# Adding P1 onto C11: 56 accumulating transfers spread over the stages after P1

## The chip, the cores and the metric

The kernel runs on one core of a Trainium2 chip. The metric is the device time of one execution in microseconds. Times are taken over several executions; the profile is one execution that was recorded by the hardware profiler.

## The reference

Eight experts each multiply the same rows by their own weights, and the results are added with softmax probabilities as factors:

```python
batch, seq, hidden, n_experts, expert_hidden = 16, 512, 512, 8, 2048
probs = np.exp(router_logits - logits_max); probs = probs / np.sum(probs, axis=-1, keepdims=True)
for e in range(n_experts):
    output += probs[:, :, e:e+1] * np.matmul(x, expert_weights[e])
```

Scaling a row of `x` by an expert's probability ahead of the product gives the same sum, so the whole is one product: 8192 rows, 8 x 512 = 4096 terms (expert and hidden), 2048 columns. Inputs and output are f32.

## The kernel before

The large product is done as a Strassen-Winograd scheme. Rows are split into blocks of 256 (`HQ`): block 2q is the "even" half, 2q+1 the "odd" one, q from 0 to 15. Experts 0 to 3 and 4 to 7 are the two halves of the terms, and the columns are split into two halves of 1024 (`NH`). Seven products P1 to P7 with sums of operands replace eight. P1 + P2 is C11, the output rows of the even block in the first half of the columns. Within each product the same scheme is used again on tiles of 128 rows and 512 columns: seven steps, in the order 1, 5, 6, 2, 7, 3, 4 (`STEPS`), each of eight matmuls into one PSUM bank. In P1, P2 and P3 most stages are opened by a third level of the scheme (`by_thirds`), in steps of four matmuls.

The work is a list of stages, `stages`, made by hand. A stage takes one or two products of one or two q; with two products it has 14 steps, called slots 0 to 13 below. The order is: seven stages of P1 (q 2 to 15), eight of P2 (q 2, 3, 4, 5, 0, 1, 6, ... in pairs), then P6 with P5 (`k5` is the first), then P7, and P4 with P7 (`k7` is the stage of the last P6 and the first P7, the turn), then P3 (`k3` is the stage of the last P4), until `end`. `ND` is 7, the first P2 stage.

TensorE runs the steps in this order. VectorE makes the left operands (tiles `z`: rows of x, `xT`, times probabilities, `pT`) and their differences (`d`), the weight sums (`w`), and most of the additions out of PSUM (`ps`, `pt`) into 128 x 512 f32 tiles `h`. ScalarE copies from PSUM into `h`. Twelve `h` buffers go round; one is free again when the transfer that stores it has landed. Of the result, some parts are added to what was stored earlier: P7 loads such a base block from the output (`h<-out_dram`) into an `h` tile.

Three queues start transfers. SP loads `xT`, `pT`, base blocks and kept operands. ScalarE's queue fetches weight sums of 1 MB (`w<-wd`). POOL stores results to the output, loads and casts weights and rows, sends weight sums to DRAM, and issues every transfer that adds onto DRAM (`accum_op=ADD`). Each queue starts its transfers in program order. A POOL transfer also waits until the one eight before it on that queue has landed.

P1's result is needed in C11 and elsewhere, so it is kept in DRAM: `kept[q]`, two column blocks of 256 rows. For q 0 to 13 (`ON_BASE` is 14) P2 stores its own part of C11 to the output, and P1 is added to it later from `kept[q]`: four transfers of 128 x 512 f32 (256 KB) each for 14 q, 56 in all, read from DRAM and added onto DRAM. The profile names them `out_dram<-kept`, the function is `add_kept`, the line of POOL's transfers is L121. They depend on nothing but P2's stores and the stores of `kept`. The hooks put them among the steps: `at(stage, slot, make)` runs `make` ahead of that step while the program is written, so the transfer gets its place on POOL's queue behind the stores of all earlier steps. Before the change, the places come from one table row each for q 0 to 11 (from stage `k7 + 3`, one q every 15 slots) and q 12, 13 (from `k3 + 5`, every 14 slots).

Of the kernel before, what the change touches and what calls it, by code (L numbers as in the profile page):

```python
# [31 lines left out]
def kernel(  # L32
# [51 lines left out]
    with tc.tile_pool(name="psum0", bufs=1, space=bass.MemoryType.PSUM) as psum0:  # L84
        zero = h_tile([P, NB], f16)
        nc.vector.memset(zero, 0.0)
        every = psum0.tile([P, 8, NB], f32, name="every")
# [32 lines left out]
    def pool(o, i, **how):  # L120
        note(nc.gpsimd.dma_start(out=o, in_=i, **how))  # L121
# [506 lines left out]
    ND = 7  # L628
    ON_BASE = 14
# [27 lines left out]
    def at(stage, slot, make):  # L657
        hooks.setdefault((stage, slot), []).append(make)

    def add(*products):  # L660
        stages.append(products)
        return len(stages) - 1
# [36 lines left out]
    def product(r, q, **how):  # L699
        left, loads = left_of(r, q)  # L700
        lefts[r, q] = left
        p = None
        if r == 1:
            def sink(tn, o):
                pool(kept_rows(q)(tn), o)
            p = Product(right[1], left, sink)
        elif r == 2:
            if q >= ON_BASE:
                bases[2, q] = Base(kept_rows(q))
            p = Product(right[2], left, to_out(q, 0, 0), bases.get((2, q)))  # L710
        elif r == 5:
            bases[6, q] = m1 = Base(kept_rows(q))
            m1.task = {}

            p = Product(right[5], left, to_out(q, 1, 0))
        elif r == 6:
            m1 = bases[6, q]

            def base(tn):
                need(m1.task[tn])  # L720
                return m1.t[tn]
            p = Product(right[6], left, to_out(q, 0, 1), base)
        elif r == 7:
            base = bases[7, q] = Base(lambda tn: out_rows(q, 0, 1, tn))
            p = Product(right[7], left, to_out(q, 1, 1), base)
        elif r == 4:
            p = Product(right[4], left, to_out(q, 1, 0, accum_op=ADD), products[7, q].o.__getitem__)
        else:
            p = Product(right[3], left, to_out(q, 0, 1, accum_op=ADD), **how)
        p.loads = loads  # L730
        products[r, q] = p
        return p
# [131 lines left out]
    k5 = add(product(5, 0), product(5, 1))  # L864
# [3 lines left out]
    some = product(6, 15)  # L868
    xs.clear()
    k7 = add(some, product(7, 0))  # L870
    for q in range(15):
        add(product(4, q), product(7, q + 1))
    some = product(4, 15)
    xs.clear()
    k3 = add(some, product(3, KEPT_Z))
    for q in range(0, KEPT_Z, 2):
        add(product(3, q), product(3, q + 1))
    end = add(product(3, 15))
# [87 lines left out]
    for i, (kn, e) in enumerate((kn, e) for kn in (ODD, (0, 0), (1, 1), (1, 0)) for e in range(2)):  # L966
        stage = ND + i - 2 if kn != ODD else 2 + 2 * i
# [42 lines left out]
    def slots_after(stage, slot, n):  # L1010
        slot += n
        while slot >= 7 * len(stages[stage]):
            slot -= 7 * len(stages[stage])
            stage += 1
        return stage, slot
# [127 lines left out]
    def add_kept(q, n, t):  # L1143
        pool(out_f[ds(2 * q * HQ + t * HP, HP), ds(n * NB, NB)], kept[q][n, ds(t * HP, HP), :], accum_op=ADD)

    for first, stage, every in ((0, k7 + 3, 15), (12, k3 + 5, 14)):
        for n, q in enumerate(range(first, min(first + 12, ON_BASE))):
            for i in range(4):
                at(*slots_after(stage, 0, every * n + every * i // 4), lambda q=q, i=i: add_kept(q, i // 2, i % 2))

    finish = products[3, 15]
    finish.base = Base(lambda tn: out_rows(15, 0, 1, tn))
# [81 lines left out]
```

## Time and profile before

| | |
|---|---|
| median of 3 runs | 1361.7 us (1361.27 to 1362.39) |
| profiled execution | 1360.91 us, of which the span from first to last instruction is 1359.1 us |
| PE busy | 1352.8 us, 6846 matmuls |
| DVE (VectorE) busy | 1133.7 us |
| ACT (ScalarE) busy | 261.4 us |
| POOL (GpSimd) busy | 435.9 us, most of it issuing transfers |
| transfers `out_dram<-kept` | 56 of 256 KB, 56.9 us of POOL, median 9.0 us from issue to landing |
| transfers `out_dram<-h` on POOL | 380 of 256 KB, median 7.5 us to landing |
| first and last `out_dram<-kept` | issued at 844.6 and 1315.8 us |

The stages lie about so in the span: P1 to 212 us, P2 to 404 us, P6 and P5 to 792 us (from 768 us the turn to P7), P7 and P4 to 1155 us, P3 to 1350 us. Busy times of engines overlap. A group of the profile has the form "line engine operation out<-in"; a releaser is what ended an idle time. The DMA share is the mean busy share of the 16 DMA engines, and it can pass 1 where packets overlap.

### The profile page before, as it was taken

The numbers are of one execution on the slowest core, as the hardware profiler recorded it, in microseconds if no ns is written. First come the engines' busy times: TensorE is split into PE (matmuls) and PEld (weight loads), VectorE is DVE, ScalarE is ACT, GpSimd is POOL, SyncE is SP. The second block draws the span as 40 slices with busy tenths as digits, with TensorE's granted clock in tenths as the row PEclk, the third lists the DMA queues.
The fourth block names the chain that finished last, engine by engine and source line by source line (L and its number), as shares of the span: only waits on it lengthen the run. The fifth ranks groups of instructions, "written<-read, shape, count | busy, mean of one in ns | idle before, by whom it ended". The sixth has DMA issues, their size and how long they took to land.

```text
span 1359.1 us, 18757 instructions
## 1 busy us (share of the span) xinstructions
PE 1352.8 (100%) x6846; PEld 667.1 (49%) x6846; DVE 1133.7 (83%) x1374; ACT 261.4 (19%) x525; POOL 435.9 (32%) x667
## 2 busy tenths in 40 slices
PE   9999999999999999999999999999999999999998
PEld 4555555565544444444444444444444444556564
DVE  7877687878999888787887899988889897898884
ACT  3232423233211111111111100000000000224331
POOL 3223323333222332323312122453434443232342
PEclk9999999999999999999999999999999999999999
DMA  9899979888899999999997998999999999999997
GB/s 186 242 221 247 258 232 233 255 243 250 238 341 288 287 310 273 288 285 284 309 274 279 345 318 236 247 267 251 264 251 249 263 265 315 327 302 251 199 163 131
DMA packets 191116, 355.65 MB, mean 262 GB/s; under 512 B 53040, under 2 KB 81968, under 8 KB 186160
## 3 DMA queue, kind: packets, MB, share of 16 engines
q0 software_dynamic: 89824, 189.31, 59.6%
q1 hardware_dynamic: 97456, 139.86, 33.5%
q10 hardware_dynamic: 3744, 25.30, 4.7%
q8 instruction: 53, 0.87, 0.3%
q14 instruction: 39, 0.32, 0.1%
HBM read 210.53 MB, written 180.55 MB: 288 GB/s over the span
## 4 chain that ended last, share of the span: by engine, by line
PE 99%; DMA 0%; DVE 0%; issue 0%; POOL 0%; ACT 0%; POOLq 0%
PE ps L130 75%; PE pt L130 24%; DMA w<-in_x_dram 0%; DVE z L255 0%; POOL w L121 0%; DVE h L107 0%; ACT h L1180 0%; DVE lg L295 0%; POOLq L1218 0%
## 5 line engine op out<-in xcount | busy, mean ns | idle before, releaser
L130 PE MATMUL ps<-w,z 128*128 128x512 f16 (+1 forms) x3776 | 821.3, 374 | 0.0
L130 PEld LDWEIGHTS <-z 128*128 128x128 f16 x5264 | 515.0, 98 | 574.4
L121 POOL DMA_DIRECT2D out_dram<-h x380 | 256.7, 710 | 684.1 <-ACT h L617 269.5
L130 PE MATMUL pt<-w,z 128*128 128x512 f16 (+1 forms) x1488 | 312.7, 357 | 0.0
L107 DVE TENSOR_TENSOR z<-xT,pT 128x2048 f16<-128x2048 f16 x220 | 265.9, 1217 | 0.8 <-DMA xT<-xs 0.8
L107 DVE TENSOR_TENSOR h<-ps,h 128x512 f32<-128x512 f32 x250 | 170.2, 687 | 88.0 <-PE ps L130 67.2
L130 PE MATMUL ps<-w,d 128*128 128x512 f16 x880 | 199.1, 379 | 0.0
L604 ACT COPY h<-ps 128x512 f32<-128x512 f32 x118 | 69.2, 586 | 417.9 <-PE ps L130 385.3
L130 PEld LDWEIGHTS <-d 128*128 128x128 f16 x880 | 86.1, 98 | 99.8
L107 DVE TENSOR_TENSOR z<-z,d 128x2048 f16<-128x2048 f16 x110 | 131.8, 1216 | 0.0
L107 DVE TENSOR_TENSOR h<-pt,h 128x512 f32<-128x512 f32 x123 | 83.5, 686 | 43.3 <-PE pt L130 41.0
L107 DVE TENSOR_TENSOR w<-w 128x1024 f16<-128x1024 f16 (+2 forms) x104 | 110.2, 1075 | 1.9 <-PE ps L130 1.0
L617 ACT COPY h<-ps 128x512 f32<-128x512 f32 x50 | 29.3, 586 | 391.5 <-PE ps L130 387.1
L107 DVE TENSOR_TENSOR ps<-ps,h 128x512 f32<-128x512 f32 (+1 forms) x90 | 51.9, 579 | 28.5 <-PE ps L130 24.9
L107 DVE TENSOR_TENSOR d<-z 128x1024 f16<-128x1024 f16 x110 | 74.7, 684 | 1.1
L600 ACT COPY h<-ps 128x512 f32<-128x512 f32 x97 | 53.8, 604 | 69.4 <-PE ps L130 65.3
L121 POOL DMA_DIRECT2D kept<-h x56 | 30.6, 548 | 93.7 <-ACT h L604 52.6
L121 POOL DMA_DIRECT2D out_dram<-kept x56 | 56.9, 1058 | 11.2 <-DMA out_dram<-h 5.8
L596 ACT COPY ps<-ps 128x512 f32<-128x512 f32 x59 | 33.6, 570 | 120.7 <-PE ps L130 62.6
L107 DVE TENSOR_TENSOR ps<-pt,h 128x256 f32<-128x256 f32 x38 | 16.4, 432 | 41.5 <-PE pt L130 29.4
L107 DVE TENSOR_TENSOR h<-h 128x512 f32<-128x512 f32 (+2 forms) x69 | 45.1, 675 | 0.6 <-DMA out_dram<-h 0.4
L107 DVE TENSOR_TENSOR z<-z,u 128x2048 f16<-128x2048 f16 x36 | 44.1, 1225 | 1.2
(74 smaller groups left out, 558.6 us busy)
## 6 DMA issues: line engine op xcount, KB each, us to landing
out_dram<-h POOLq DMA_DIRECT2D x380, 256.0 KB, 7.5
pT<-p_dram SPq DMA_DIRECT2D x126, 256.0 KB, 7.7
w<-wd ACTq DMA_DIRECT2D x23, 1024.0 KB, 9.4
xT<-x SPq DMA_DIRECT2D x80, 256.0 KB, 7.7
h<-kept SPq DMA_DIRECT2D x72, 256.0 KB, 7.7
h<-out_dram SPq DMA_DIRECT2D x68, 256.0 KB, 6.7
w<-in_expert_weights_dram POOLq DMA_DIRECT2D x33, 512.0 KB, 10.3
kept<-h POOLq DMA_DIRECT2D x56, 256.0 KB, 6.0
```

The lines of the kernel that those rows point to most:

```text
L107: dve(nc.vector.tensor_tensor(out=o, in0=a, in1=b, op=op))
L121: note(nc.gpsimd.dma_start(out=o, in_=i, **how))
L130: note(nc.tensor.matmul(ps, z, w, start=start, stop=stop, skip_group_check=True))
L596: act(nc.scalar.copy(self.banks["b"], x))
L600: act(nc.scalar.copy(o[tn], q if p == 5 else x))
L604: act(nc.scalar.copy(o[TN[p]], b if p == 2 else x))
L617: act(nc.scalar.copy(o[tn], b))
```

## The change

The table of places is replaced. The 56 transfers are the same, on the same queue, with the same sources and targets. Their order is now q 2, 3, 4, 5, 0, 1, 6, ..., 13, the order in which P2 stores them, and the places are listed by stage and slot: two a stage in five stages of P2, two a stage in six of the stages of P6 with P5, alternately two and one a stage in P7 with P4 (from the first stage after the turn), two a stage in P3 from `k3 + 2`. 57 places are listed and the last is not used.

```diff
-    for first, stage, every in ((0, k7 + 3, 15), (12, k3 + 5, 14)):
-        for n, q in enumerate(range(first, min(first + 12, ON_BASE))):
-            for i in range(4):
-                at(*slots_after(stage, 0, every * n + every * i // 4), lambda q=q, i=i: add_kept(q, i // 2, i % 2))
+    added = [(q, i) for q in (2, 3, 4, 5, 0, 1, 6, 7, 8, 9, 10, 11, 12, 13) for i in range(4)]
+    places = [(stage, slot) for some, slots in (
+        (range(ND + 2, ND + 7), (3, 10)), ((k5 + 5, k5 + 7, k5 + 9, k5 + 10, k5 + 12, k5 + 13), (4, 11)),
+        (range(k7 + 1, k3, 2), (2, 9)), (range(k7 + 2, k3, 2), (6,)), (range(k3 + 2, end), (4, 10))) for stage in some for slot in slots]
+    for (q, i), where in zip(added, sorted(places)):
+        at(*where, lambda q=q, i=i: add_kept(q, i // 2, i % 2))
+    assert len(places) >= len(added)
```

The order of the instructions on TensorE, VectorE, ScalarE and SP is the same as before. On POOL it differs in the place of the adds alone. `kept_145` is the kept tile of q 2, `kept_143` that of q 0, `kept_144` of q 1, `kept_149` of q 6, `kept_148` of q 5.

POOL in a stage of P2, before:

```order
L121 DMA w<-in_expert_weights_dram 128x4x512 x2
L121 DMA wd<-u 128x2048
L121 DMA wd<-w 128x2048 x2
L121 DMA out_dram<-h 128x512 x8
L121 DMA w<-in_expert_weights_dram 128x4x512 x2
```

And with the change:

```order
L121 DMA w<-in_expert_weights_dram 128x4x512 x2
L121 DMA out_dram<-kept_145 128x512
L121 DMA wd<-u 128x2048
L121 DMA wd<-w 128x2048 x2
L121 DMA out_dram<-h 128x512 x4
L121 DMA out_dram<-kept_145 128x512
L121 DMA out_dram<-h 128x512 x4
```

One add now stands ahead of the sends of the weight sums, one amid the eight stores.

POOL from the end of P6 with P5 over the turn to P7 into P7 with P4, before (the stores are those of three stages and more):

```order
L121 DMA wd<-w 128x1024
L121 DMA out_dram<-h 128x512 x8
L121 DMA xs<-in_x_dram 128x2x512
L121 DMA out_dram<-h 128x512 x48
L121 DMA out_dram<-kept_143 128x512 x2
L121 DMA out_dram<-h 128x512
```

And with the change:

```order
L121 DMA xs<-in_x_dram 128x2x512
L121 DMA out_dram<-kept_144 128x512
L121 DMA out_dram<-h 128x512 x5
L121 DMA out_dram<-kept_144 128x512
L121 DMA out_dram<-h 128x512 x27
L121 DMA out_dram<-kept_144 128x512
L121 DMA out_dram<-h 128x512 x3
L121 DMA out_dram<-kept_144 128x512
L121 DMA out_dram<-h 128x512 x5
L121 DMA out_dram<-kept_149 128x512
```

Where 48 stores followed each other ahead of the first add, there are now adds ahead of the first store and after 5, 32, 35 and 40 of them. The add after 32 stores is the first in the stage after the turn; before the change the first add of all stands 16 stores behind that place.

## The prediction

> **What bounds the kernel now.** I read the page's busy row first, then the chain of waits, then the busy time by stage, since a mean over the whole span could hide an idle stretch where the adds stand. The first fence has the page's head, PE's busy tenths over 40 slices and the chain; the second has five windows that cover the program from P1 to P3 (columns: stretch, length, then busy time of PE, PEld, DVE, ACT and POOL, the granted clock, the DMA share, GB/s).
>
> ```profile
> span 1359.1 us, 18757 instructions
> ...
> PE   9999999999999999999999999999999999999998
> ...
> PE 99%; DMA 0%; DVE 0%; issue 0%; POOL 0%; ACT 0%; POOLq 0%
> ```
>
> ```profile
> 24.00:212.00 188.00, 188.00 (x1051) 101.97 (x1049) 146.34 (x175) 64.52 (x136) 53.11 (x88) 1.00 0.99 236
> 212.00:404.00 192.00, 192.00 (x1058) 103.25 (x1056) 159.07 (x186) 57.46 (x123) 55.86 (x97) 1.00 0.93 264
> 404.00:792.00 388.00, 388.00 (x1799) 175.90 (x1798) 324.76 (x392) 53.47 (x92) 106.52 (x188) 1.00 0.98 296
> 792.00:1155.00 363.00, 363.00 (x1683) 164.59 (x1682) 321.93 (x384) 17.59 (x30) 146.51 (x201) 1.00 1.02 262
> 1155.00:1350.00 195.00, 195.00 (x1099) 107.35 (x1097) 163.00 (x200) 61.14 (x132) 62.65 (x73) 1.00 1.00 235
> ```
>
> The windows are P1, P2, P6 with P5, P7 with P4, and P3. In every one the PE time equals the length of the stretch: TensorE has no idle time from 24 us to 1350 us, at the full clock. The start before 24 us and the stores after the last matmul hold no add. So in this execution there is nothing for another order of transfers to win; it can only lose, by making TensorE wait somewhere. The fourth row holds 48 of the 56 adds today, and even there PE is full. POOL is busy at most 146.51 of 363.00 us, so it has room for more issues in any stage.
>
> **The change, part by part.** No transfer is added or taken away; 56 adds of 256 KB leave their places and take others on the same queue. Their cost to POOL and their flight, from the view of the tile over 840 to 1150 us (min/median/max ns of the issue, then landing), beside the plain stores of P2:
>
> ```profile
> L121 POOL DMA_DIRECT2D out_dram<-kept x48: 805/916/1501, 844.6 to 1145.9; - x48
> ...
> DMA to landing us min/median/max: 5.7/9.0/14.9
> ...
> L121 POOL DMA_DIRECT2D out_dram<-h x32: 540/540/548, 264.5 to 346.7; - x32
> ...
> DMA to landing us min/median/max: 2.6/4.2/6.2
> ```
>
> POOL's queue. Counted in the new table, 10 adds go to P2, 12 to P6 and P5, 23 to P7 and P4, 11 to P3. The issues cost 10 x 0.92 = 9.2 us of POOL in P2, where 192.00 - 55.86 = 136 us are free, and 12 x 0.92 = 11 us in P6 and P5, where 388.00 - 106.52 = 281 us are free. P7 and P4 give back 25 x 0.92 = 23 us. What stands behind an add on POOL is a store of `out_dram`, a send `wd<-u` or, in P6 and P5, a part of a weight load; each goes out at most one add later, 0.8 to 1.5 us. Who waits for those stores is told by the view of the tile `out_dram`: for 264 to 352 us its part "who waited for it" is empty, so a store of P2 that lands in 4.2 us is not missed by anyone if it lands 1.5 us later. On ScalarE, which needs the `h` tiles that the stores give back, that stretch has these waits and no others, all on TensorE or VectorE:
>
> ```profile
> ACT h L604 <- PE ps L130: 45.9, 16, 8.0
> ACT ps L596 <- DVE ps L107: 9.0, 7, 1.9
> ACT h L600 <- PE ps L130: 3.1, 3, 1.0
> ```
>
> Term for P2: 0; if that cover were gone, 10 x 0.92 = 9.2 us. Term for P6 and P5: 0 by the same argument, but with less behind it: there the tile's view has some waits on the landing of a store.
>
> ```profile
> L121 POOL DMA_DIRECT2D out_dram<-h x107: 540/540/630, 406.3 to 719.0; - x107
> ...
>   ACT h L604: 19.5, 2
>   ACT h L600: 2.9, 1
> ...
>   DVE h L107: 1.5, 2
> ```
>
> ScalarE is busy 53 of 388 us there, and its two long waits (19.5 us together) stand in a run in which PE is full; so waits of 10 us on that side are covered. Uncovered, 12 x 0.92 = 11 us. The last add ahead of the turn to P7 stands in the third stage before it, and no add is placed in the turn itself, so the tight handover of weights there is left as it is.
>
> The two stages after the turn to P7. The present table leaves them free: its first add is at 844.6 us. The new one puts two adds in the first of them and one in the second. Counting 16 stores back from the present first add, the first new add stands behind the pair at 794.37, and the second behind the store at 808.77 and ahead of that at 810.50:
>
> ```profile
> 794.37 1.14 POOL L121 DMA_DIRECT2D out_dram<-h  x2 [3.59 <-DVE h L107]
> ...
> 808.77 0.86 POOL L121 DMA_DIRECT2D out_dram<-h  x1 [1.28 <-DVE h L107]
> 810.50 0.56 POOL L121 DMA_DIRECT2D out_dram<-h  x1 [0.87 <-DVE h L107]
> ```
>
> This is the one place where I find little room. The timelines of SP, DVE and PE there:
>
> ```profile
> 810.12 1.78 SPq L118 DMA_DIRECT2D h<-out_dram  x4
> ...
> 817.17 0.69 DVE L107 TENSOR_TENSOR h<-ps,h 128x512 f32<-128x512 f32 x1 [1.05 <-DMA h<-out_dram]
> 817.78 1.22 DVE L107 TENSOR_TENSOR z<-xT,pT 128x2048 f16<-128x2048 f16 x1
> 818.92 1.22 DVE L107 TENSOR_TENSOR u<-xT,pT 128x2048 f16<-128x2048 f16 x1
> 820.17 1.22 DVE L107 TENSOR_TENSOR z<-z,u 128x2048 f16<-128x2048 f16 x1
> 821.31 1.29 DVE L107 TENSOR_TENSOR ps<-ps,h 128x512 f32<-128x512 f32 x2
> ...
> 823.12 3.62 PE L130 MATMUL ps<-w,d 128*128 128x512 f16 x16
> ```
>
> VectorE already waits 1.05 us for the base block of P7 that SP asked for at 810.12. From there it runs without a gap to the first `ps<-ps,h`, which reads the bank of step 1 and ends at 821.31 + 0.69 = 822.00. Step 6 writes on in that bank at 823.12. So the load may be late by 823.12 - 822.00 = 1.1 us before TensorE stands still, and from there on every microsecond is one of the end. Now the add flies beside that load. What a flying add does to such a load is read from the DMA view (count, size, median us to landing) in three windows: 806 to 826 us, with no add; 850 to 900 us, with 8 adds; 870 to 886 us, where the loads met the most adds:
>
> ```profile
> h<-out_dram SPq DMA_DIRECT2D x4, 256.0 KB, 7.3
> ...
> h<-out_dram SPq DMA_DIRECT2D x8, 256.0 KB, 9.1
> ...
> h<-out_dram SPq DMA_DIRECT2D x4, 256.0 KB, 11.7
> ```
>
> Bounds of the lateness: 0 from below, and 11.7 - 7.3 = 4.4 us from above; the stall is that less 1.1, so 0 to 3.3 us. The value taken: 8 adds in 50 us (one in 6 us) cost 9.1 - 7.3 = 1.8 us; two adds in a stage of 24 us (one in 12 us) are half as dense, so I take 0.9 us, 0.2 us short of the room. Term: 0.
>
> The Trainium skill, page "DMA: Bandwidth & Descriptors", section "Issuing engines are not separate DMA queues", speaks against the change at this very place: transfers started by different engines run on the same 16 DMA engines and interleave. The rows 7.3 and 9.1 agree with that. The same page's "Anatomy of one DMA — SWDGE (gpsimd) path" fits a transfer as 2.0 us and its bytes over 436e3 per us, which makes an estimate of 2.6 us for 256 KB; if the whole add came ahead of the load, TensorE would stand 2.6 - 1.1 = 1.5 us and the time would be 1363.2. The landing of 9.0 us in the trace does not agree with 2.6 us.
>
> The rest of P7 and P4. 25 adds fewer in the stretch with the highest DMA share (1.02). Waits for adds end there on POOL's own queue, as `POOL out_dram L121`, `POOL w L121` and `POOL wd L121`; they become rarer. PE is full now, so this gives 0.
>
> P3. 11 adds instead of 8, beginning three stages earlier. Stores here land late, and one wait of ScalarE shows:
>
> ```profile
> L121 POOL DMA_DIRECT2D out_dram<-h x52: 853/856/1869, 1199.8 to 1343.6; - x52
> ...
>   ACT h L604: 1.1, 1
> ...
> DMA to landing us min/median/max: 3.1/8.0/17.8
> ```
>
> The 8 adds of today stand in the same kind of stage, beside a full PE. Term 0; uncovered, 11 x 1.1 = 12 us.
>
> Sum: 0 + 0 + 0 + 0 + 0. Against the profiled execution (1360.9 us, of which 1359.1 are span) that is 1360.9; the median of the runs shown, 1361.7, lies 0.8 above it, and with nothing gained or lost the new median is 1361.7.
>
> **Rivals.** What a measurement of this kernel can tell from no change is about 0.2%, 2.7 us.
>
> The load at 810 us comes later than I take it (slower). One place, one price: the stall is the landing less 8.4 us (7.3 + 1.1). At the 11.7 of the densest window it is 3.3 us, 1365.0; it passes 2.7 us from a landing of 11.1 us. For it: VectorE is already waiting for that very load. Against: three adds or more overlapped the loads of that window, here it is one, with the other 15 us earlier. Chance 0.07 for over 2.7 us; smaller stalls belong to my forecast.
>
> P3's queue gets longer (slower). Its stages are written as thirds, in which ScalarE's copies into `h` free banks for TensorE; a store that lands behind an add keeps an `h` tile. The price is one wait of 1.1 us for each of 11 adds, 12 us, 1374. It decides once a store lands later than ScalarE's turn to the same buffer; the single 1.1 us wait says that this happens at the edge, and PE 195.00 of 195.00 says that it did not reach TensorE with adds in the last stages. Chance 0.05.
>
> The thinner traffic in P7 and P4 pays (faster). In the profiled execution there is nothing to regain. If the 0.8 us by which the median is above it are waits in that stretch, they could go: 1360.9, still within 0.2%. More than 2.7 us would have to come from idle time that the windows exclude. Chance 0.03.
>
> That the transfers do not move is excluded: the new order of POOL's queue shows them in the new places.
>
> **How the numbers follow.** Forecast: no change, 1361.7, chance 0.85 with all stalls below 2.7 us. Slower 0.07 + 0.05 = 0.12, faster 0.03. The range goes from 1360.4 (the 0.8 us regained, and half a microsecond for the spread of the runs) to 1365.2 (the upper bound 3.3 us of the one unknown price on the median, with 0.2 for spread); P3's 1374 and the larger gain stay outside, about 1 in 10.
>
> **What would show it.** Right: PE still full in all five windows; adds at about 255 us first and 1321 us last; a DVE wait on `h<-out_dram` near 817 us that grows from 1.05 to about 2 us, with the `ps<-w,d` group still at 823.1. Wrong: a PE group there that starts late and shifts all behind it; ScalarE rows in P2 or P3 that wait on `out_dram<-h` or `out_dram<-kept` ahead of a PE gap; a time above 1365 with gaps in P6 and P5, which would mean that loads there had less room than PE's full row let me see.

## The result and the profile after

The changed kernel takes 1374.1 us (median of 11 runs, 1363.5 to 1383.3), the kernel before 1362.0 us beside it (11 runs, 1361.1 to 1363.7). The ratio is 1.0081, with a 95% interval of 1.0063 to 1.0099: slower by about 0.8%, 12 us at the median, where no change was forecast. Repeated in a later set of runs, the same kernel took 1364.2 us (11 runs, 1361.2 to 1382.2), ratio 1.0011 [1.0002, 1.0020].

The spread belongs to the result. None of the runs of the kernel before, in any set, was above 1364.9 us; of the changed kernel 10 of 11 were above 1365 in the first set and 3 of 11 in the second. The ratios leave out runs more than 1.5% above a kernel's fastest (three runs below, 1382 to 1387 us), so I give beside each ratio how many of all runs were above 1365 us.

The profiled execution took 1367.6 us, 6.7 more than that of before. First its page: the span, TensorE's busy tenths, the busy share of the transfer engines over the 40 slices, and the chain of waits by engine.

```profile
span 1365.4 us, 18734 instructions
...
PE   9999999999999999999999999999999999999998
...
DMA  9899989999999999999999999899998989999987
...
PE 90%; issue 5%; DMA 2%; DVE 1%; POOL 1%; SPq 0%; POOLq 0%; ACT 0%; DVEq 0%
```

The same row of transfer engines in the page of the kernel before:

```profile
DMA  9899979888899999999997998999999999999997
```

TensorE's row of tenths tells nothing: a stall of 2.5 us disappears in a slice of 34. The chain is no longer "PE 99%", and in the transfer engines' row the eights of P2 (slices 8 to 11) and the 7 in slice 22 have become nines. The windows say where the time went (columns as in the prediction: length, busy time of PE, PEld, DVE, ACT, POOL, clock, DMA share, GB/s):

```profile
212.00:404.00 192.00, 192.00 (x1057) 103.32 (x1056) 156.64 (x186) 57.58 (x122) 65.30 (x107) 1.00 1.03 274
404.00:792.00 388.00, 382.87 (x1774) 173.35 (x1772) 320.27 (x385) 53.72 (x92) 115.49 (x196) 1.00 1.07 301
792.00:1155.00 363.00, 362.87 (x1682) 164.33 (x1681) 324.79 (x387) 17.59 (x30) 122.17 (x174) 1.00 0.93 242
1155.00:1350.00 195.00, 195.00 (x1099) 107.36 (x1098) 163.88 (x200) 61.14 (x132) 69.05 (x81) 1.00 1.02 247
```

P2 and P3 are full, P7 with P4 lost 0.13 us, P6 with P5 lost 388.00 - 382.87 = 5.13 us. There the DMA share rose from 0.98 to 1.07. (Together that is 5.3 of the 6.3 us by which the span is longer; the last 1.0 us lies in the first 24 us, before any add.) TensorE's timeline shows two stalls, and VectorE's shows what it waited for ahead of them:

```profile
737.00 3.18 PE L130 MATMUL ps<-w,z 128*128 128x512 f16 x14 [2.32 <-DVE h L107]
...
781.15 2.10 PE L130 MATMUL ps<-w,d 128*128 128x512 f16 x9 [2.56 <-DVE ps L107]
```

```profile
723.29 1.29 DVE L107 TENSOR_TENSOR h<-h 128x512 f32<-128x512 f32 x2 [3.42 <-DMA h<-kept]
...
732.65 0.69 DVE L107 TENSOR_TENSOR h<-h 128x512 f32<-128x512 f32 x1 [2.21 <-DMA h<-kept]
...
776.39 1.90 DVE L107 TENSOR_TENSOR h<-h 128x512 f32<-128x512 f32 x3 [5.41 <-DMA h<-kept]
```

The chain is the same in both: a load `h<-kept`, asked for by SP, lands late; VectorE waits in order behind it; TensorE waits for VectorE's next result. So the loss arises on SP's queue, which the change does not touch. Its own waits in 500 to 800 us (us in total, times, longest), before and then with the change:

```profile
SPq L118 <- DMA z<-z: 4.2, 2, 2.9
...
SPq L118 <- DMA pT<-p_dram: 3.2, 1, 3.2
...
SPq L118 <- DMA h<-kept: 0.3, 1, 0.3
```

```profile
SPq L118 <- DMA xT<-xs: 16.4, 8, 4.9
SPq L118 <- DMA z<-z: 15.4, 6, 4.8
SPq L118 <- DMA pT<-p_dram: 15.2, 5, 5.6
...
SPq L118 <- DMA h<-kept: 13.5, 7, 3.8
```

SP issues in order. In the program its transfers and ScalarE's loads take turns on eight semaphores, so that each waits for the one eight before it. The tiles `xs`, `xT` and `pT` also share ten buffers, so that a load of `pT` can have to wait until the transposes `xT<-xs` have read the `xs` tile whose buffer it takes. SP's waits on its own transfers, 7.7 us before in these rows, are 60.5 us now, and the one on transposes did not occur before. In the same two views its waits for the work of others (stores `out_dram<-h`, casts `xs<-in_x_dram`, VectorE's `z`) fell from 65.6, 59.4 and 37.0 us to 46.8, 46.5 and 16.6: SP was early before, and that slack is used up. The waits on its own transfers become long because the transfers do. The view of transfers in 500 to 790 us (count, size, median us from issue to landing; for the queue q0, POOL's, packets, MB, share of 16 engines), before and then with the change:

```profile
q0 software_dynamic: 14330, 35.64, 41.8%
...
h<-kept SPq DMA_DIRECT2D x43, 256.0 KB, 7.4
z<-z SPq DMA_DIRECT2D x19, 512.0 KB, 8.8
...
xT<-x SPq DMA_DIRECT2D x15, 256.0 KB, 7.4
...
xT<-xs SPq DMA_TRANSPOSE x18, 3.7
```

```profile
q0 software_dynamic: 15984, 38.54, 52.7%
...
h<-kept SPq DMA_DIRECT2D x44, 256.0 KB, 10.3
...
z<-z SPq DMA_DIRECT2D x19, 512.0 KB, 12.0
...
xT<-x SPq DMA_DIRECT2D x15, 256.0 KB, 12.8
out_dram<-kept POOLq DMA_DIRECT2D x12, 256.0 KB, 12.6
...
xT<-xs SPq DMA_TRANSPOSE x18, 8.4
```

With twelve adds in this stretch the loads shown land 3 to 5 us later at the median. As an estimate from these rows, eight in flight that take 12 us instead of 8 are a queue that can pass two thirds as much.

### The profile page after: what moved, and what is told of

Same layout as the page of the kernel before. It is cut to its first block, busy times and chain, and to the rows that moved or that the text cites. A ratio compares the mean times of both kernels' runs of the same rounds, so it can differ in the third digit from the quotient of the medians.

```text
span 1365.4 us, 18734 instructions
## 1 busy us (share of the span) xinstructions
PE 1353.3 (99%) x6846; PEld 666.8 (49%) x6846; DVE 1132.4 (83%) x1374; ACT 261.5 (19%) x525; POOL 437.2 (32%) x667
## 4 chain that ended last, share of the span: by engine, by line
PE 90%; issue 5%; DMA 2%; DVE 1%; POOL 1%; SPq 0%; POOLq 0%; ACT 0%; DVEq 0%
PE ps L130 69%; PE pt L130 21%; POOL out_dram L121 1%; DMA out_dram<-h 1%; DMA h<-out_dram 1%; DMA w<-in_expert_weights_dram 1%; DVE z L107 1%; DVE h L107 0%; DVE ps L107 0%; DVE d L107 0%; POOL w L121 0%; SPq L118 0%; POOLq L121 0%; ACT h L1183 0%; DVEq L107 0%
## 5 line engine op out<-in xcount | busy, mean ns | idle before, releaser
L121 POOL DMA_DIRECT2D out_dram<-h x380 | 252.7, 701 | 706.1 <-ACT h L617 291.2
L600 ACT COPY h<-ps 128x512 f32<-128x512 f32 x97 | 53.8, 604 | 70.1 <-PE ps L130 65.6
L107 DVE TENSOR_TENSOR ps<-pt,h 128x256 f32<-128x256 f32 x38 | 16.4, 433 | 41.5 <-PE pt L130 29.4
```

The costliest lines, as they stand in the source:

```text
L107: dve(nc.vector.tensor_tensor(out=o, in0=a, in1=b, op=op))
L600: act(nc.scalar.copy(o[tn], q if p == 5 else x))
```

## The experiments

All kernels differ from the two of the case in the table of places alone, or in transfers added at places of that table. "12 adds" below are those at the six stages of P6 and P5.

| what is run | median us (lowest to highest) | ratio to before, 95% | runs above 1365 |
|---|---|---|---|
| the change without adds in P6 and P5 | 1363.3 (1362.0 to 1367.2) | 1.0011 [1.0002, 1.0021] | 2 of 10 |
| the 12 adds alone | 1366.2 (1361.5 to 1377.6) | 1.0040 [1.0010, 1.0069] | 6 of 10 |
| the 12 adds alone, again | 1367.9 (1361.3 to 1376.9) | 1.0049 [1.0026, 1.0073] | 7 of 12 |
| three adds behind the turn alone | 1362.0 (1361.1 to 1362.9) | 0.9999 [0.9990, 1.0009] | 0 of 10 |
| ten adds in P2 alone | 1363.1 (1361.0 to 1366.2) | 1.0005 [0.9996, 1.0015] | 1 of 10 |
| P2 and the 12 | 1363.0 (1361.7 to 1371.0) | 1.0015 [1.0004, 1.0027] | 2 of 12 |
| the 12 and three behind the turn | 1362.1 (1361.0 to 1387.1) | 1.0020 [0.9998, 1.0041] | 5 of 12 |
| all up to the turn (25 adds) | 1364.0 (1361.7 to 1382.4) | 1.0021 [1.0002, 1.0041] | 3 of 12 |
| the changed kernel again | 1364.2 (1361.2 to 1382.2) | 1.0011 [1.0002, 1.0020] | 3 of 11 |
| first 8 of the 12 | 1362.1 (1361.1 to 1367.6) | 1.0002 [0.9994, 1.0011] | 1 of 11 |
| last 4 of the 12 | 1361.7 (1361.1 to 1364.2) | 1.0002 [0.9993, 1.0010] | 0 of 11 |
| 12 tiny copies besides | 1361.5 (1360.6 to 1364.6) | 0.9998 [0.9990, 1.0007] | 0 of 11 |
| 12 copies of 256 KB besides | 1361.3 (1360.4 to 1362.7) | 0.9994 [0.9986, 1.0003] | 0 of 11 |
| 12 such copies in rows of 2 KB | 1361.6 (1360.6 to 1363.5) | 0.9999 [0.9990, 1.0007] | 0 of 11 |
| 24 such copies | 1364.6 (1361.1 to 1370.6) | 1.0024 [1.0008, 1.0040] | 6 of 12 |
| 11 adds, begun earlier | 1372.2 (1363.3 to 1375.1) | 1.0066 [1.0043, 1.0089] | 5 of 6 |
| the 12 at slots 4 and 13 | 1370.3 (1363.4 to 1383.9) | 1.0079 [1.0050, 1.0108] | 9 of 10 |
| the change, the 12 at 4 and 13 | 1364.2 (1361.7 to 1364.9) | 1.0012 [1.0003, 1.0020] | 0 of 11 |

### Which part of the change

The theory was by then the lag on SP's queue in P6 and P5; the rivals were the forecast's own suspect (the two stages behind the turn) and P2. The edits, in parts of their lines with (...) for what is left out: the changed kernel with its twelve adds of P6 and P5 at further places in P7 and P4, and the table of before with the first adds moved to one piece of the new places.

```diff
-((k5 + 5, k5 + 7, k5 + 9, k5 + 10, k5 + 12, k5 + 13), (4, 11)),
+(range(k7 + 2, k3, 2), (12,)), (range(k7 + 3, k7 + 13, 2), (6,)),
```

```diff
+    old = [slots_after(stage, 0, every * n + every * i // 4) for first, stage, every, of in ((0, k7 + 3, 15, 12), (12, k3 + 5, 14, 2))
+           for n in range(of) for i in range(4)]
+    moved = [(stage, slot) for some, slots in (...) for stage in some for slot in slots]
+    places = moved + old[len(moved):]
```

> The changed kernel with the 12 adds of P6 and P5 moved into P7 and P4 (35 there instead of 23); the 10 in P2, the three in the two stages after the turn and those in P3 stay. Backlog theory (the 12 adds take the spare transfer time of P6 and P5, SP's loads fall up to 15 us behind and the turn to P7 waits): back to 1361.5 to 1363. After-the-turn theory (the three adds that meet P7's base load): stays at 1368 to 1378. P2 theory (adds in P2 leave something late): stays above 1368.

> The kernel before with 12 adds alone moved into the places in P6 and P5; the other 44 stay in the old table's places. Backlog theory: the whole loss, 1368 to 1380, with PE gaps between 720 and 790 us. The two other theories: 1361 to 1363.

> The kernel before with three adds alone moved into the two stages after the turn (the new places at about 796, 810 and 826 us). Backlog theory: 1361 to 1363. After-the-turn theory: 1368 to 1378. My prediction's price for this place was a stall of 0 to 3.3 us.

> The kernel before with the first 10 adds alone moved into P2. Backlog theory: 1361 to 1363, since P2's stores land in 4.2 us and nothing waits for them. P2 theory: above 1368.

Without the adds in P6 and P5, 1.3 of the 12 us are left; with them alone, six of ten runs are above 1365. The three adds behind the turn cost nothing, and P2's ten no more than can be told from nothing. So most of the loss arises in P6 and P5. The 1.3 us are clear of nothing by their interval, so a small part has another source, which I did not find. What did not fit: 4.2 + 1.1 + 0.0 is 5.3 us and not 12.

### Whether the pieces act on each other

The same table, with two and with all three pieces moved; and the changed kernel again, beside them.

> The table of before with the first 22 adds moved: 10 to the places in P2, 12 to those in P6 and P5; the first stages of P7 hold none. Alone, the 12 cost 4.2 us (1366.2) and the 10 cost 1.1 us (1363.1); all of the change costs 12 us. Theory 'the two pieces before the turn act on each other' (both make SP late ahead of the same turn): 1370 to 1374, that is the whole loss without any add behind the turn. Theory 'they only add up': 4.2 + 1.1 = 5.3 us, about 1367.3, and the other 7 us of the loss must then come from behind the turn.

> The table of before with the first 15 adds moved: 12 to the places in P6 and P5, three to the first two stages after the turn; P2 holds none. Theory 'the lag that P6 and P5 leave on SP's queue is still there behind the turn, and the adds there keep it from being caught up': 1370 to 1374 although the three alone cost nothing. Theory 'they only add up': 4.2 + 0.0, about 1366.2.

> The table of before with the first 25 adds moved as the change has them: 10 in P2, 12 in P6 and P5, three in the first two stages after the turn; the other 31 stay in the old places. Theory 'three pieces together make the turn late': close to what all of the change gives beside it. Theory 'the rest of P7, P4 and P3 has a part of the loss': no more than the 4 us that the 12 adds of P6 and P5 cost alone, about 1366.

> The changed kernel once more, on the same chip as the three runs beside it. Theory 'the loss is the kernel's': 1370 to 1378 as before. Theory 'a part of it is the chip's' (P2 with P6 and P5 gave only 1363.0 on another chip than the 1366.2 of P6 and P5 alone): 1363 to 1368.

No combination gives the 12 us, and in this later set the changed kernel itself gave 2.2 us. The medians of these kernels say little: each has runs at 1361 to 1362 and runs at 1370 to 1387. What they share is that some runs go wrong, that is, end above 1365 us. The theory of an interaction (1370 to 1374) falls, and so does that of a sum (1367.3 and 1366.2): the first two gave 1363.0 and 1362.1. How often a run goes wrong was not the same from set to set; why is open (below).

### Adds against copies

Three kernels leave the 56 adds as before and put other transfers at the 12 places: one row of 2 KB; 256 KB onto unbroken memory; 256 KB in rows 8 KB apart, as an add writes them. A fourth puts two of the last kind for each add. The edit of the third:

```diff
+    spare = dram.tile([3, HP, 4 * NB], f32, name="spare")
+    for n, (stage, slot) in enumerate([(stage, slot) for stage in (k5 + 5, k5 + 7, k5 + 9, k5 + 10, k5 + 12, k5 + 13) for slot in (4, 11)]):
+        at(stage, slot, lambda n=n: pool(spare[n // 4, :, ds(n % 4 * NB, NB)], kept[2 + n // 4][n % 4 // 2, ds(n % 2 * HP, HP), :]))
```

> The kernel before with its 56 adds where they are, and besides them 12 copies of one row of 2 KB at the 12 places in P6 and P5: they take POOL's issue time and a place on its queue, and nearly no bytes. Theory 'bytes': 1362.0, no gap on TensorE, landings as before. Theory 'place on POOL's queue' (a store or a weight load that goes out one issue later, or waits for the transfer eight before it): 1364 to 1368 as with the adds.

> The kernel before with its 56 adds where they are, and besides them 12 plain copies of the same size (256 KB, DRAM to DRAM, to a spare buffer, no accumulation) at the 12 places in P6 and P5. Work is added. Theory 'bytes': the transfer engines are full there, so 12 more transfers of 256 KB delay SP's loads like the adds do, 1364 to 1368, landings of SP's loads in 575 to 745 us of 10 us and more. Theory 'the accumulation is what costs' (adds of f32 onto DRAM are slow at the transfer engines): 1362 to 1363, landings near before's 7 to 9 us.

> The kernel before with its 56 adds where they are, and 12 plain copies of 256 KB at the 12 places in P6 and P5, now written as an add is, in rows of 2 KB that lie 8 KB apart in a spare buffer. Copies onto unbroken memory cost nothing (1361.3) and took 36 packets each by the packet counts of POOL's queue, where an add takes some 137. Theory 'small packets': 1364 to 1368 with landings of SP's loads above 10 us in 500 to 790 us, POOL's queue 8 points or more above the 41.8% of before. Theory 'the accumulation': 1361 to 1362.5, landings of 7 to 9 us, POOL's queue at about 45% as with the unbroken copies.

> The kernel before with its 56 adds where they are, and 24 plain copies of 256 KB in rows of 2 KB, two at each of the 12 places in P6 and P5. From the shares of POOL's queue in 500 to 790 us, 12 copies took 3.1 points (144 us of packet time, 12 us each), 8 adds 5.2 points (30 us each) and 12 adds 6.1 to 8.2 points (24 to 32 us each) where nothing stood still. Theory 'time of the transfer engines': 24 copies take as much as 12 adds, so they lose as these do: runs up to 1377 and a median of 1363 to 1367. Theory 'the accumulation itself': no loss, 1361.3 to 1362.3, no run above 1365.

POOL's issue time and the places on its queue are free (tiny copies), and so are 12 more transfers of 256 KB. The accumulation is what differs, but not as a thing of its own: 24 copies lose like 12 adds. What is common shows in POOL's share of the transfer engines in 500 to 790 us, in four kernels whose TensorE was little held up in the profile (not at all in the first three, 4.3 us in the last): with 12 copies in rows, 4 adds, 8 adds and 24 copies, in this order.

```profile
q0 software_dynamic: 15304, 38.84, 44.9%
```

```profile
q0 software_dynamic: 14945, 36.85, 44.7%
```

```profile
q0 software_dynamic: 15488, 37.76, 47.0%
```

```profile
q0 software_dynamic: 16167, 41.65, 50.8%
```

Over the 41.8% of before, and with 290 us x 16 engines = 4640 us of packet time: 12 copies take 3.1 points, 12 us each; 4 adds 2.9 points, 34 us each; 8 adds 5.2 points, 30 us each; 24 copies 9.0 points, 17 us each. (These differences also hold what the load does to POOL's other packets.) The same sum for the three kernels with all 12 adds that were hardly held up (47.9% in the changed kernel's second set, 48.7% in P2 and the 12, 50.0% in the 12 and three behind the turn) gives 24, 27 and 32 us an add. So an add of 256 KB occupies the transfer engines for about as long as two copies. The kernels can then be put in the order of their DMA share in 500 to 750 us. The rows of before, of 12 copies in rows, of 24 copies and of the 12 adds (second set):

```profile
500.00:750.00 250.00, 250.00 (x1160) 113.33 (x1159) 205.28 (x253) 36.19 (x62) 70.83 (x125) 1.00 0.94 283
```

```profile
500.00:750.00 250.00, 250.00 (x1160) 113.32 (x1159) 205.23 (x253) 36.17 (x62) 77.45 (x137) 1.00 0.98 296
```

```profile
500.00:750.00 250.00, 246.40 (x1142) 111.64 (x1141) 201.51 (x249) 35.59 (x61) 84.00 (x149) 1.00 1.05 305
```

```profile
500.00:750.00 250.00, 237.78 (x1091) 107.19 (x1089) 194.64 (x240) 34.73 (x60) 78.41 (x130) 0.97 1.07 277
```

In the same view the other kernels stand at 0.96 (last 4 adds), 1.02 (first 8), 1.02 to 1.05 (P2 and the 12; the 12 and the turn; the changed kernel again) and 1.07 to 1.08 (the changed kernel; the 12 alone, first set; all up to the turn). With transfers added or moved in P6 and P5 alone, up to 0.98 no run was above 1365 (the tiny copies, both kernels with 12 copies, the last 4 adds); of all that have some there, two sets at 1.02 have 1 and 2 such runs, and from 1.04 up all sets but one have three or more. This goes with the load and does not prove it as the cause. Each share is that of one execution, and a part of the order is that execution's own: the changed kernel stood at 1.07 in one profile and at 1.05 in the other. Nor does the share alone decide it: the exception, the last kernel below, stands at 1.07.

The Trainium skill, page "DMA: Bandwidth & Descriptors", section "Issuing engines are not separate DMA queues", says that transfers started by different engines share the same 16 DMA engines; the traces agree, since a table that only POOL sees slowed `xT<-x` of SP from 7.4 to 12.8 us.

### Nearness to the turn, number, or the meeting with transposes

> The table of before with the first 8 adds moved, to the first four of the six stages in P6 and P5; the last four (720 us and later) are not there. Theory 'lag on SP's queue that is not caught up before the turn': the quieter 60 us ahead of the turn let SP catch up, 1362 to 1362.5. Theory 'each add costs by itself wherever it stands': two thirds of the 4.2 us, about 1364.8.

> The table of before with the first 4 adds moved to the last two of the six stages in P6 and P5. Theory 'closeness to the turn': these four carry the loss, some runs at 1366 to 1377, median above 1363. Theory 'lag that builds up over all 12': four make no lag that matters, 1361.5 to 1362.5 and no run above 1365.

> The table of before with the first 12 adds moved into P6 and P5, but into the stages k5 + 1, 3, 5, 7, 9, 10, so that none stands in the last 60 us ahead of the turn. Theory 'lag that is not caught up before the turn': SP catches up, 1361.5 to 1362.5, no more than one run above 1365. Theory 'number': as with the 12 at the places of the change, median 1362 to 1366 with runs up to 1377.

> The 12 adds of P6 and P5 alone, as in the second run, once more beside the three above. Theory 'the loss is the kernel's, and every run draws anew whether SP comes late': between 2 and 7 of 11 runs above 1365, the lowest at 1361 to 1362. Theory 'the loss was of one chip': no run above 1365.

Eight cost nothing and four cost nothing, and twelve cost 4 to 6 us: neither the nearness to the turn nor a price per add. The third run needs care: stage `k5 + 1` has no slot 11, so one of the 12 adds was left out, and the kernel does 55 of 56. With 11 adds in P6 and P5, the last at 657 us and thus none in the last 110 us ahead of the turn, it was slower still. Its profile has six stalls of TensorE of 0.4 to 3.1 us from 486 to 672 us, and none from there to the turn. So my theory of a lag that only the turn brings to light falls: TensorE was hit while the adds were going out, and a quiet stretch ahead of the turn comes too late for that.

What happens in a bad run stands in the profile of the 12 adds' second set, where TensorE stood still for 12 us. Rows of PE, DVE and SP (start, length; the time in brackets is the idle time ahead), and the windows around:

```profile
722.23 6.25 PE L130 MATMUL ps<-w,z 128*128 128x512 f16 x16 [12.22 <-DVE h L107]
```

```profile
717.89 0.69 DVE L107 TENSOR_TENSOR h<-h 128x512 f32<-128x512 f32 x1 [11.09 <-DMA h<-kept]
```

```profile
699.00 17.52 SPq L118 DMA_DIRECT2D pT<-p_dram  x2
```

```profile
690.00:700.00 10.00, 10.00 (x48) 4.58 (x47) 4.26 (x7) 0.85 (x2) 5.11 (x9) 1.00 1.13 317
700.00:709.00 9.00, 9.00 (x44) 4.05 (x43) 6.76 (x8) 0.31 (x1) 0.53 (x1) 1.00 1.17 144
```

From 699 us SP issues nothing for 17 us. Its next load, the second `pT<-p_dram` of that row, waits for the two transposes `xT<-xs` ahead of it, as SP's view of 500 to 800 us shows (us in total, times, longest):

```profile
SPq L118 <- DMA xT<-xs: 31.5, 9, 16.2
```

Meanwhile the transfer engines are full (1.17) and move 144 GB/s, where they moved 317 ten microseconds earlier. The view of transfers in 700 to 717 us has half of the packets under 512 bytes, and an add that took 27 us to land:

```profile
DMA packets 1708, 2.85 MB, mean 168 GB/s; under 512 B 881, under 2 KB 1053, under 8 KB 1600
...
out_dram<-kept POOLq DMA_DIRECT2D x1, 256.0 KB, 27.0
```

By the trace, the two transposes `xT<-xs` issued at 693 and 694 us landed 20 and 22 us later. They were not alone: five stores issued in 692 to 700 us landed in 20.3 us at the median, and SP's loads in 21 to 27. In the timelines of the 12 adds and of the changed kernel, the adds at slot 11 go out 0.3 to 9 us behind a transpose, about half of them within 3.5. The theory was that they meet there. So the last pair moved only those to slot 13:

```diff
-((k5 + 5, k5 + 7, k5 + 9, k5 + 10, k5 + 12, k5 + 13), (4, 11)),
+((k5 + 5, k5 + 7, k5 + 9, k5 + 10, k5 + 12, k5 + 13), (4, 13)),
```

> The 12 adds of P6 and P5 alone (as in the second run), with the second add of each stage at slot 13 instead of 11, so that it is issued about 6 to 8 us behind the pair of transposes xT<-xs instead of 2 to 4 us; number, size and stages are the same. Theory 'adds that meet the transposes': the transposes land in 3 to 7 us again, 1361.5 to 1362.5, no more than one run above 1365. Theory 'sum of the transfers': as the 12 adds twice before (6 of 10 and 7 of 12 runs above 1365, medians of 1366.2 and 1367.9).

> The changed kernel with only that difference: the second adds of the six stages in P6 and P5 at slot 13 instead of 11. Theory 'adds that meet the transposes': about as with no adds in P6 and P5, 1363.3, no more than two or three runs above 1365. Theory 'sum of the transfers': 1364 to 1374 as the changed kernel in its two sets.

The meeting as cause falls. With the 12 adds alone it got worse, 1370.3 us, and the transposes landed later than ever, though the moved adds stood 5 to 14 us behind the last of them:

```profile
h<-kept SPq DMA_DIRECT2D x43, 256.0 KB, 13.1
...
xT<-xs SPq DMA_TRANSPOSE x18, 11.5
```

With the whole change it gave 1364.2 us and no run above 1365, as that theory would have it. I have no reason for the opposite signs; the only difference ahead of 790 us is that in the whole change P2 has done ten adds, and so the adds of P6 and P5 belong to other rows of the output.

SP's wait on transposes parts the profiles more sharply than the share does. In 500 to 800 us it was at most 8.9 us in every profile in which TensorE waited 2.2 us or less there (8.9 in this last kernel), and 16.4 to 31.5 us in all seven in which TensorE waited 4.3 us or more (16.4 in the changed kernel, 21.6 with 24 copies, 31.5 in the profile above). Late transposes may be the link through which a crowded stretch stops SP, or one more sign of the crowding; no run takes this wait away, so it is not shown as the cause.

## Why the prediction was wrong

**What bounds the kernel: right, and too weakly read.** TensorE was full, and only losses were possible. But the same windows held the DMA share, 0.98 at 296 GB/s in P6 and P5, 1.02 at 262 GB/s in P7 and P4, and I took POOL's free time as the room for an add. The room that counts is on the transfer engines and on SP's queue.

**P2, term 0: right** within what can be told (1.0005 [0.9996, 1.0015]; PE 192.00 of 192.00 with the share at 1.03). One thing is unexplained: the profiled run of that kernel, its slowest at 1366.2 us, has a stall of 2.2 us at the turn, where VectorE waits 5.1 us for `h<-out_dram`, though no add went out from 366 to 911 us.

**P6 and P5, term 0: the step that failed.** It rested on "the same argument, but with less behind it": POOL's 281 free us and ScalarE's covered waits. The uncovered price of 11 us was that of POOL's queue, and the tiny copies show that POOL's queue costs nothing; that 11 lies near the measured 12 is luck. What the runs show in its place is 12 adds of some 24 to 34 us of packet time each in a stretch already at 0.94 to 0.98. Where time was lost, most of SP's loads landed in 10 to 15 us instead of 7 to 9, its in-order queue stood behind its own late transfers, VectorE waited for `h<-kept`, TensorE for VectorE: 5.1 us in the profile, 4 to 8 us at the median of the three sets with the 12 alone (slot 13 among them), 12 and 2 us for the whole change. The last criterion of the prediction, a time above 1365 with gaps in P6 and P5, is what came.

**The two stages behind the turn: place and size right, and not the cause.** With the three adds alone VectorE's wait for the base block grew from 1.05 to

```profile
819.34 0.69 DVE L107 TENSOR_TENSOR h<-ps,h 128x512 f32<-128x512 f32 x1 [2.27 <-DMA h<-out_dram]
```

2.27 us, about the 2 us foretold, and TensorE lost next to nothing: 1362.0 us. The bounds for that stall, 0 to 3.3 us, held in the profiles too; the longest, 1.6 us, came in the change without adds in P6 and P5. I had put all doubt there, since it was the one place where an add stands beside a load with little room in the timeline. In P6 and P5 no single load had little room in the trace of before; the room was lost by all of them together.

**P7 and P4, P3: right.** 0.13 us lost in the first, none in the second. That P3's stores would hold ScalarE (the 1374 us rival) did not happen, though the number came near the result by accident.

**The range** (to 1365.2) was built on the only price I left open. The price of the adds in P6 and P5 was never bounded from above by the rows nearest to it: the DMA view at 870 to 886 us, which I quoted for the turn, had `h<-out_dram` at 11.7 us beside dense adds, and the same +4 us on the loads of P6 and P5 would have made that stage a rival.

## What to carry to other kernels

A queue's free issue time says nothing about the room for a transfer; read the DMA share of the stage, the landing times of the loads that the bounding engine needs, and what their issuing queue waits for; and count an accumulating transfer as about two copies, as it came out here. Where a stage stands at a share near 1 with TensorE full, work that seems to hide anywhere can use up the slack of an in-order load queue, and then a run's time scatters: look at the spread of the runs before the median. Place such transfers where the loads have slack, which need not be the stage with the lowest use of the issuing engine.

## What was not expected of the hardware

**A stall can cost twice, by where it falls.** The clock of TensorE changed only in steps of about 3.41 us: each stretch at 0.5 ahead of the program's end lasted 3.4, 6.8 or 13.7 us. With windows laid on these steps, counted from the first rise to full clock at about 5 us, ten adds in P2 alone (first fence) and 24 copies (second) compare:

```profile
776.90:780.30 3.40, 1.36 (x7) 0.49 (x5) 0.64 (x2) 0.00 (x0) 0.00 (x0) 1.00 0.87 301
780.30:783.70 3.40, 3.29 (x8) 1.14 (x8) 3.40 (x6) 0.00 (x0) 0.00 (x0) 0.50 0.85 241
```

```profile
732.30:735.70 3.40, 1.38 (x7) 0.52 (x6) 2.73 (x4) 0.86 (x2) 1.08 (x2) 1.00 0.96 358
735.70:739.10 3.40, 1.82 (x9) 0.87 (x9) 3.37 (x5) 0.00 (x0) 0.00 (x0) 1.00 0.98 350
739.10:742.50 3.40, 3.40 (x18) 1.51 (x17) 3.40 (x4) 0.00 (x0) 0.25 (x1) 1.00 1.03 402
```

In the first, a stall of 2.2 us left TensorE busy for 1.36 of 3.40 us, and the next window ran at half clock, 8 matmuls instead of 17, which adds some 1.7 us. In the second, a stall of 3.6 us lay over two windows, 1.38 and 1.82 us busy, and the clock stayed. The two stalls of 2.3 and 2.6 us in the changed kernel's profile lay over two windows each and did not lower it either. In the profiles of this case, from 24 us on, a window with 1.36 us busy or less was followed by one at half clock, a full-clock window with 1.38 us or more was not. At the start of one profile (the change without adds in P6 and P5) a window with 1.48 us busy, of short matmuls of 128 columns, was followed by one at half clock as well. So it is an observation of a bound near 0.4, and not a law. A window that was itself at half clock needed more: after two that were busy for about 0.6 of their length, the next was still at half. The Trainium skill, page "TensorE: Matmul & The Clock Gate", section "Part 1: The HAM clock gate (the "warmup" mystery)", describes such a free-running window of 3.4 us; the trace agrees with its length. The Trainium skill's section "HAM oscillation — how this bites in real kernels" on the same page gives the rule that no idle gap should exceed about 3.4 us. The measurements differ from it: here 2.2 us were enough, and 3.6 us were not.

**The full transfer engines can move half as much.** 144 GB/s at a share of 1.17 against 317 GB/s at 1.13 ten microseconds earlier. The changed kernel's profile has such a stretch too, 144 GB/s at 0.99 from 720 to 730 us. Half of the packets in the first were small ones (881 of 1708 under 512 bytes, in a stretch with two transposes in flight). But the same piece of the program in the kernel before, 680 to 697 us, has nearly as many (1312 of 2837) and moves 251 GB/s, and the two slot-13 kernels speak against each other; what triggers it is open.

**What stays open.** Why the changed kernel lost 12 us in one set and 2 us in another. It need not be the chip: the 12 adds alone lost alike on two chips (6 of 10 and 7 of 12 runs above 1365). What P2's ten adds ahead of the 12 do is open too. The 12 alone had 22 of 32 runs above 1365 (at slots 4 and 11 or 13); with P2's ten ahead, four sets had 2 of 12, 3 of 12, 3 of 11 and 0 of 11, but the first set of the changed kernel had 10 of 11. No version tried beats the kernel before.
